# A hybrid mLSTM/GLA block with a PEER feed-forward: all activations computed ahead of the dense stage

## The chip, the core and the metric

The kernel runs on one core of a Trainium2 chip. The time is device microseconds of one execution of the whole program. The kernel before took 3271.71 us in the median of three runs (3260.62 to 3278.69).

## The reference, cut to what matters

One trunk layer over 1024 tokens of width 1024: a token mixer (two scans, mLSTM and gated linear attention, in both directions), and then a product-key feed-forward layer, PEER, whose experts are single neurons. The change is inside PEER and behind it.

```python
PEER_HEADS, PEER_NKEYS, PEER_TOPK = 8, 128, 16        # 128 * 128 = 16384 experts
def retrieve(xb):                                     # xb: 128 tokens x 1024
    q = (xb @ wq).reshape(128, 8, 2, 128)
    s = jnp.einsum('tphq,phkq->tphk', q, keys)        # 128 scores per head and half
    top_s, top_i = lax.top_k(s, 16)
    cand = top_s[:, :, 0, :, None] + top_s[:, :, 1, None, :]
    best_s, best_c = lax.top_k(cand.reshape(128, 8, 256), 16)
    ...
    idx = i1 * 128 + i2                               # 128 experts for each token
    g = jax.nn.softmax(best_s, axis=-1)
    act = jax.nn.gelu(jnp.einsum('tpkd,td->tpk', u_tab[idx], xb))
    return jnp.einsum('tpk,tpkd->td', g * act, v_tab[idx])
...
x = x + g2 * peer_ffn(h2, ...)
return rms_norm(x, norm_f_g)
```

Each token so uses 128 of the 16384 rows of U and of V, each 1024 long, in float32.

## The kernel before, in words

The front of the program (adaLN, projections, the scans, the output projection) runs to about 780 us and is the same in both kernels. PEER, function `peer`, then treats the eight blocks of 128 tokens in two ways.

*Gathered blocks.* Three blocks (`ng` = 3) fetch their rows. One **gather step** serves one of the 128 experts of each of 128 tokens: an indirect DMA on the POOL queue (L936) brings 128 rows of 8 KB (U and V side by side) into one of four buffers `uv`; VectorE multiplies the U half by the tokens and sums (L983, the dot); ScalarE applies gelu and the gate to one column `act` (L948, L949); VectorE adds `act` times the V half to the sum `acc` (L961, the add). There are 384 steps. In the query stage of the dense blocks every second dot's product is made by POOL (`share`, L981) and summed by ScalarE. The sum stands in PSUM (`accP`) up to the dense stage, and from there on in SBUF (`acc`).

*Dense blocks.* The other five blocks (640 tokens, `nd`) compute all experts, in 128 chunks of 128. For each chunk TensorE multiplies U by the 640 tokens (tile `ua`, 48 matmuls, each value as a high and a low float32r part, three products), ScalarE applies gelu (`w`); a table of gates G, made from the selected indices by one-hot matmuls (tile `gb`) and stored in DRAM as `d_G`, is multiplied in (L1376); the product is split into `wh` (ScalarE, L1379) and `wl` (VectorE, L1380); and TensorE multiplies it by V, half a row of 1024 at a time (L1403, tile `po`).

*Stages.* (1) queries and selection of the gathered blocks, to about 987 us; (2) queries and selection of the dense blocks, to 1370; (3) the table G, 80 pieces of 8 tokens, to 1832; (4) the last of the early activations; (5) the dense stage, from 1868 us. 84 of the 128 chunks (`early`) have their activations computed ahead of (5) and stored in DRAM as `d_A`; the other 44 are computed inside it.

*The order* is written out by the code itself; there is no scheduler in this part. A generator (`gather_all`) yields one gather step at a time. `dve(us, rate)` is called with an estimate of the VectorE work just recorded; it credits `rate` gather steps per microsecond, and records as many as are due (`ticks`). `fill` then records activation matmuls (a second generator) until an estimated TensorE clock is `lead` ahead of an estimated VectorE clock. So `rho` (query stage and selection), `rhog` (table) and `sige` (last activations) say how many gather steps stand beside each stage's work, and what is left of the 398 steps is spread over the dense stage: `share_of` per microsecond of matmul, times `ratio` in rounds of the first half of D.

*The dense stage.* Groups of 8 chunks (`GRP`) accumulate in PSUM: a **round** is one group and one half of D, five banks, one for each token block. In a round of the second half the weights of the next group are produced beside the matmuls (`produce`, `weights`). At the end of a round each bank is added to `accB` in SBUF (`v_add`: L1410, VectorE; in group 0 a copy by ScalarE, L1408). Six banks belong to these rounds and two to the `ua` products; so the second tile of a round needs a bank that the round before must have emptied. V arrives in pieces of 128 x 512 (`v_load`, L1348), ScalarE and POOL split each (`vh`, L1368, `vl`, L1369). U arrives in two halves per chunk (L1032), split by L1042 and L1043.

## Time and profile before

| | |
|---|---|
| median of three runs | 3271.71 us |
| profiled execution, its own time | 3258.37 us |
| its span, first to last instruction | 3256.6 us |
| mean granted TensorE clock | 0.945 |
| TensorE busy | 2895.9 us, 89% |
| VectorE busy | 2583.2 us, 79% |
| GpSimd busy | 1581.0 us, 49% |
| ScalarE busy | 1304.8 us, 40% |
| moved by DMA | 831.44 MB, mean 255 GB/s |

Busy time is the time in which an engine executes; what it waited for is shown by other views. Busy shares are averages over stages that differ, so the rows below are read by stage. Columns are explained where a view first appears.

### The profile page before, as it was taken

How to read it: one execution, taken by the hardware profiler on the slowest of the kernel's cores; microseconds unless marked ns; L12 is line 12 of the kernel's file. 1: busy time of each engine (PE TensorE's matmuls, PEld its weight loads, DVE VectorE, ACT ScalarE, POOL GpSimd, SP SyncE). 2: the span in 40 equal slices, each digit the busy share in tenths (PEclk: the TensorE clock that was granted, in tenths of full speed). 3: DMA queues.
4: the chain of work that ended last, by engine and by line, in shares of the span. 5: the costliest groups of instructions: out<-in, count | busy, mean ns of one | idle time of the engine just before them, and what ended most of it. 6: DMA issues, size and time to landing. Idle time of an engine off the chain costs nothing.

```text
span 3256.6 us, 47765 instructions
## 1 busy us (share of the span) xinstructions
PE 2895.9 (89%) x17321; PEld 2560.1 (79%) x17321; DVE 2583.2 (79%) x4467; ACT 1304.8 (40%) x2909; POOL 1581.0 (49%) x1102
## 2 busy tenths in 40 slices
PE   6999989998988987798888889989998899999897
PEld 3899887777988987688887877777777777778775
DVE  6633418666898999999999778888888788888886
ACT  4622224453444455455555433333333233333232
POOL 1000002333456766644343466666665566667664
PEclk9999999799998998899999999999999899999999
DMA  5254437345377876689898999999988898999883
GB/s 204 71 182 143 142 110 261 123 134 178 120 261 267 286 261 238 218 283 322 314 320 310 353 318 318 315 319 310 311 301 308 302 321 305 321 315 320 305 294 126
DMA packets 374381, 831.44 MB, mean 255 GB/s; under 512 B 27001, under 2 KB 198649, under 8 KB 324737
## 3 DMA queue, kind: packets, MB, share of 16 engines
q0 software_dynamic: 57600, 411.07, 35.0%
q1 hardware_dynamic: 292624, 347.74, 33.6%
q10 hardware_dynamic: 23920, 69.59, 5.5%
q8 instruction: 136, 2.23, 0.3%
q14 instruction: 101, 0.82, 0.1%
HBM read 729.38 MB, written 98.91 MB: 254 GB/s over the span
## 4 chain that ended last, share of the span: by engine, by line
DVE 21%; issue 11%; PE 10%; POOL 9%; DMA 5%; ACT 1%; SPq 0%; POOLq 0%; DVEq 0%; ACTq 0%
PE po L1403 7%; POOL vl L1369 4%; DVE ol L1296 4%; POOL uv L936 4%; DVE uv L983 4%; PE ua L1017 3%; DVE acc L961 3%; DMA uv<-uv,idx 3%; DVE accP L961 2%; DVE oh L1297 2%; DVE oh L1295 2%; DVE o L1294 2%; DVE w L1376 1%; DMA vr<-uv 1%; ACT wh L1379 1%
## 5 line engine op out<-in xcount | busy, mean ns | idle before, releaser
L936 POOL DMA_INDIRECT uv<-uv,idx x384 | 512.9, 1336 | 548.2 <-DVE accP L961 237.3
L983 DVE SCALAR_TENSOR_TENSOR uv<-uv,h2a 128x1024 f32<-128x1024 f32 x351 | 543.9, 1550 | 106.7 <-DMA uv<-uv,idx 106.5
L1403 PE MATMUL po<-vh,wh 128*128 128x512 f32 x1255 | 509.5, 406 | 118.4 <-DVE accB L1410 106.0
L1403 PE MATMUL po<-vl,wh 128*128 128x512 f32 x1255 | 507.1, 404 | 16.4 <-POOL vl L1369 16.4
L1017 PE MATMUL ua<-hBhi,uh 128*128 128x320 f32 x2048 | 487.2, 320 | 36.9 <-ACT uh L1042 30.3
L1403 PE MATMUL po<-vh,wl 128*128 128x512 f32 x1255 | 503.8, 401 | 0.0
L1017 PE MATMUL ua<-hBhi,ul 128*128 128x320 f32 x2048 | 478.4, 315 | 21.2 <-POOL ul L1043 20.9
L1369 POOL TENSOR_TENSOR vl<-vr,vh 128x512 fp32r<-128x512 f32 x251 | 387.2, 1545 | 198.4 <-ACT vh L1368 177.9
L1017 PE MATMUL ua<-hBlo,uh 128*128 128x320 f32 x2048 | 477.1, 315 | 0.0
L1043 POOL TENSOR_TENSOR ul<-ur,uh 128x512 fp32r<-128x512 f32 x256 | 391.9, 1553 | 171.3 <-ACT uh L1042 164.4
L961 DVE SCALAR_TENSOR_TENSOR acc<-uv,act,acc 128x1024 f32<-128x1024 f32 x237 | 398.3, 1681 | 8.5 <-ACT act L949 8.5
L1403 PEld LDWEIGHTS po<-vh,wh 128*128 128x128 f32 x1255 | 246.2, 196 | 179.8 <-DVE accB L1410 115.4
L1017 PEld LDWEIGHTS ua<-hBhi,uh 128*128 128x128 f32 x2048 | 352.0, 194 | 44.3 <-ACT uh L1042 32.9
L1017 PEld LDWEIGHTS ua<-hBhi,ul 128*128 128x128 f32 x2048 | 351.3, 193 | 26.9 <-POOL ul L1043 26.9
L1017 PEld LDWEIGHTS ua<-hBlo,uh 128*128 128x128 f32 x2048 | 352.6, 193 | 0.0
L1403 PEld LDWEIGHTS po<-vl,wh 128*128 128x128 f32 x1255 | 246.3, 196 | 72.0 <-POOL vl L1369 22.3
L1403 PEld LDWEIGHTS po<-vh,wl 128*128 128x128 f32 x1255 | 245.5, 196 | 53.0
L1379 ACT ACTIVATE wh<-w 128x640 fp32r<-128x640 f32 x128 | 94.6, 739 | 465.5 <-DVE w L1376 465.5
L1368 ACT ACTIVATE vh<-vr 128x512 fp32r<-128x512 f32 x251 | 156.5, 625 | 186.7 <-PE po L1403 156.1
L948 ACT ACTIVATE act<-act 128x1 f32<-128x1 f32 x384 | 76.1, 198 | 353.8 <-DVE uv L983 352.1
L468 POOL MEMSET v<- 128x4 f32 x20 | 2.0, 105 | 419.1 <-PE tm L207 383.7
L1380 DVE TENSOR_TENSOR wl<-w,wh 128x640 fp32r<-128x640 f32 x128 | 113.3, 885 | 104.8 <-ACT wh L1379 100.8
(375 smaller groups left out, 5920.5 us busy)
## 6 DMA issues: line engine op xcount, KB each, us to landing
ur<-uC SPq DMA_DIRECT2D x256, 256.0 KB
vr<-uv SPq DMA_DIRECT2D x256, 256.0 KB
d_G<-gtl ACTq DMA_DIRECT2D x80, 512.0 KB
gch<-d_G SPq DMA_DIRECT2D x64, 640.0 KB
d_A<-w ACTq DMA_DIRECT2D x84, 320.0 KB
w<-d_A SPq DMA_DIRECT2D x84, 320.0 KB
wm<-w_mod SPq DMA_DIRECT2D x32, 512.0 KB
qraw<-wq SPq DMA_DIRECT2D x32, 512.0 KB
```

Of the source, the lines that this page charges most:

```text
L936: G.indirect_dma_start(out=t.rearrange("p a d -> p (a d)"), out_offset=None, in_=A["uv"], in_offset=bass.IndirectOffsetOnAxis(ap=idxs[n][: ...
L948: S.activation(acts[i], acts[i], AF.Gelu)
L961: V.scalar_tensor_tensor(acc, v, act, acc, op0=ALU.mult, op1=ALU.add)
L983: V.scalar_tensor_tensor(t, t, 1.0, h2s[n], op0=ALU.mult, op1=ALU.mult, accum_out=acts[i])
L1017: T.matmul(pt[:, :b - a], l[:, kt], m[:, kt, a:b], start=(kt == 0 and wi == 0), stop=(kt == KT - 1 and wi == 2))
L1043: G.tensor_tensor(ul[:, k], ur, uh[:, k].bitcast(F32), op=ALU.subtract)
L1296: V.tensor_tensor(ol, oh, pairs(glT, b, t0), op=ALU.mult)
L1368: S.activation(vh, vr[n], AF.Copy)
L1369: G.tensor_tensor(vl, vr.pop(n), vh.bitcast(F32), op=ALU.subtract)
L1379: S.activation(wh, w, AF.Copy)
L1380: V.tensor_tensor(wl, w, wh.bitcast(F32), op=ALU.subtract)
L1403: T.matmul(po, st[:, b * P:(b + 1) * P], m, start=(start and wi == 0), stop=(stop and wi == 2))
```

## The change

- All 128 chunks have their activations computed ahead of the dense stage and stored in `d_A`; `early` and the code for the other case are gone. Those that are left after the table stage follow it in one loop. The dense stage multiplies by V alone.
- `GRP` = 8 becomes `GROUPS` = seven groups of 16 and two of 8.
- The sums of the gathered blocks stay in PSUM to the end: the two banks of `accP` belong to the whole function, in place of the two for `ua` in the dense stage.
- U is loaded and split a whole chunk at a time (128 x 1024), V two chunks of one half at a time (a new array `vC`, 4 KB runs), and G four chunks at a time.
- The first loads of the dense stage (three `d_A`, one G, three V) are issued ahead of the last activations.
- `weights` becomes a generator: w and wh first, wl at the next call.
- rho 0.42 to 0.58, rhog 0.33 to 0.43, ratio 1.35 to 4.0.

```diff
-GRP = 8
-NX = 5
+GROUPS = [16] * 7 + [8, 8]
+NX = 6
...
-def peer(tc, A, F, order, ng, out, ahi, alo, eh, ga, h2s, h2_load, early=84, rho=0.42, rhog=0.33, ratio=1.35, lead=6.0, sige=0.2):
+def peer(tc, A, F, order, ng, out, ahi, alo, eh, ga, h2s, h2_load, rho=0.58, rhog=0.43, ratio=4.0, lead=6.0, sige=0.2):
...
     def u_load(c):
-        if c < ulim[0] and c not in us:
-            us[c] = []
-            for k in (0, 4):
-                ur = ru[0].tile([P, 4, P], F32, tag="ru", name="ur")
-                Y.dma_start(ur, A["uC"][plan[c]][:, k:k + 4])
-                us[c].append(ur)
+        if c < P:
+            us[c] = ru.tile([P, KT, P], F32, tag="ru", name="ur")
+            Y.dma_start(us[c], A["uC"][c])
...
+    def activations():
...
+        for c in range(P):
+            pts = [bank("ua") for _ in cuts]
+            for n, d in enumerate(project(pts, None, *us.pop(c), bhi, blo, cuts)):
+                if n == 0:
+                    u_prep(c + 1)
+                if n == 1:
+                    u_load(c + 3)
+                yield d
+            w = up.tile([P, nd], F32, tag="we", name="w", bufs=3)
+            for pt, (a, b) in zip(pts, cuts):
+                S.activation(w[:, a:b], pt[:, :b - a], AF.Gelu)
+            S.dma_start(d_A[c], w)
...
-    owed, spare = [0.0], [(early - 4) * KT // 2]
+    owed, spare = [0.0], [(P - 4) * KT // 2]
...
+        pc = es.enter_context(tc.tile_pool(name="pc", bufs=1, space=PSUM))
         pb = esp.enter_context(tc.tile_pool(name="pb", bufs=6, space=PSUM))
-        pc = esp.enter_context(tc.tile_pool(name="pc", bufs=1, space=PSUM))
...
+    for c in range(3):
+        a_load(c)
+    g_load(0)
+    for n in range(0, 6, 2):
+        v_load(n)
+    for d in earlier:
+        clock["PE"] += d
+        ticks(d, sige)
+    v_prep(0)
     eru.close()
...
-    for n in list(accs):
-        if accs[n] is psum[0]:
-            settle(n)
-    psum.clear()
...
             V.tensor_tensor(w3, w3, gts[c // 4][:, :, c % 4], op=ALU.mult)
             wh = wp.tile([P, nd], F32R, tag="wh", name="wh")
+            S.activation(wh, w, AF.Copy)
+            yield
             wl = wp.tile([P, nd], F32R, tag="wl", name="wl")
-            S.activation(wh, w, AF.Copy)
             V.tensor_tensor(wl, w, wh.bitcast(F32), op=ALU.subtract)
...
         def produce(c):
...
-            if c not in first:
-                for d in u_side(plan.index(c), True):
-                    ticks(d, share_of)
-            pend.append(c)
+            a_load(c + 3)
+            if c % 4 == 0:
+                g_load(c + 4)
+            pend.append(weights(c))
...
-        share_of = max(steps[0] - 12, 0) / (ratio * mm + mm + (P - early) * KT * 3 * nd / 2400.0)
+        some = sum(GROUPS[:-1]) + GROUPS[0]
+        many = sum(GROUPS[1:-1])
+        share_of = max(steps[0] - 12, 0) / ((ratio * many + some) * nb * t1)
...
+                rate = share_of * (ratio if g and not h else 1.0)
...
+    A['vC']=f(i['peer_v'][0].reshape(64,2,128,2,512).transpose(0,3,2,1,4))
```

What this does to the order is seen in the built programs. Counted there, of the 384 adds of the gather steps 77 stand before the table stage, 62 in it, 9 from there to the first weights and 236 behind them; after the change 105, 82, 44 and 153. Of the 128 chunks of activations 79 stand before the end of the table stage, 8 more before the first V matmul, and 41 behind it; after it 94.25, 33.75 and none.

VectorE in the dense stage before the change, from the end of a second-half round into a first-half round (`uv` and `acc` rows are a gather step's dot and add, `gch` a part of G, `po` a bank):

```order
L1376 TENSOR_TENSOR w_22056<-w_22056,gch_22058 128x640
L1380 TENSOR_TENSOR wl_22214<-w_22056,wh_22213 128x640
L1410 TENSOR_TENSOR accB_19123<-accB_19123,po_21750 128x512
L1410 TENSOR_TENSOR accB_19123<-accB_19123,po_21751 128x512
L1410 TENSOR_TENSOR accB_19123<-accB_19123,po_21752 128x512
L1410 TENSOR_TENSOR accB_19123<-accB_19123,po_21753 128x512
L1410 TENSOR_TENSOR accB_19123<-accB_19123,po_21754 128x512
L983 SCALAR_TENSOR_TENSOR uv_22131,act_22245<-uv_22131,h2a_17103 128x1024
L961 SCALAR_TENSOR_TENSOR acc_19127<-uv_22063,act_22172,acc_19127 128x1024
L1376 TENSOR_TENSOR w_22093<-w_22093,gch_22058 128x640
L1380 TENSOR_TENSOR wl_22259<-w_22093,wh_22258 128x640
L983 SCALAR_TENSOR_TENSOR uv_22168,act_22275<-uv_22168,h2a_17103 128x1024
```

The same engine after the change, where the weights of a second-half round end and the gather steps of a first-half round begin (`accP` is the sum in PSUM):

```order
L1363 TENSOR_TENSOR wl_22934<-w_22837,wh_22926 128x640
L983 SCALAR_TENSOR_TENSOR uv_22726,act_22958<-uv_22726,h2a_14968 128x1024
L961 SCALAR_TENSOR_TENSOR accP_8048<-uv_22632,act_22829,accP_8048 128x1024
L1358 TENSOR_TENSOR w_22865<-w_22865,gch_22758 128x640
L983 SCALAR_TENSOR_TENSOR uv_22825,act_22983<-uv_22825,h2a_14968 128x1024
L961 SCALAR_TENSOR_TENSOR accP_8048<-uv_22726,act_22958,accP_8048 128x1024
L1363 TENSOR_TENSOR wl_22986<-w_22865,wh_22971 128x640
L983 SCALAR_TENSOR_TENSOR uv_22954,act_23007<-uv_22954,h2a_14968 128x1024
L961 SCALAR_TENSOR_TENSOR accP_8048<-uv_22825,act_22983,accP_8048 128x1024
L983 SCALAR_TENSOR_TENSOR uv_22979,act_23032<-uv_22979,h2a_14968 128x1024
L961 SCALAR_TENSOR_TENSOR accP_8048<-uv_22954,act_23007,accP_8048 128x1024
```

From there the gather steps go on without another instruction between them to the five adds of `po`: between two such adds stand 17 gather steps and one weight, or 5 gather steps and 15 weights, by turns. Before, the two kinds had 6 or 7 and 1, or 8 to 10 and 7.

SP's queue at the end of the table stage, before the change (`ur` is U, `w<-d_A` stored activations, `gch` G, `vr` V):

```order
L909 DMA out<-ft 128x1024
L1032 DMA ur<-uC 128x512 x10
L1340 DMA w<-d_A 128x640
L1032 DMA ur<-uC 128x512 x2
L1334 DMA gch<-d_G 128x10x128
L1348 DMA vr<-uv 128x512 x5
```

And after it:

```order
L909 DMA out<-ft 128x1024
L1027 DMA ur<-uC 128x1024 x30
L1312 DMA w<-d_A 128x640 x3
L1306 DMA gch<-d_G 128x10x256
L1319 DMA vr<-vC 128x1024 x3
L1027 DMA ur<-uC 128x1024 x31
```

The first loads of the dense stage stood behind the early chunks' U; now 31 loads of U follow them.

## Rows read from the trace of the kernel before

**Rows 1.** The page: busy time, share of the span and instructions of each engine.

```profile
PE 2895.9 (89%) x17321; PEld 2560.1 (79%) x17321; DVE 2583.2 (79%) x4467; ACT 1304.8 (40%) x2909; POOL 1581.0 (49%) x1102
```

**Rows 2.** Busy time by stage: stretch, length, engines, clock, DMA share, GB/s.

```profile
987.00:1155.00 168.00, 160.75 (x1097) 157.99 (x1098) 159.57 (x710) 78.71 (x199) 122.45 (x74) 0.98 0.80 280
1155.00:1370.00 215.00, 163.87 (x996) 157.54 (x995) 210.83 (x529) 105.72 (x217) 139.74 (x91) 0.88 0.70 241
1370.00:1832.00 462.00, 400.34 (x3320) 385.47 (x3320) 454.99 (x518) 265.20 (x459) 192.31 (x148) 0.96 0.87 307
1832.00:1868.00 36.00, 34.44 (x235) 34.18 (x234) 17.18 (x20) 13.92 (x37) 21.30 (x16) 1.00 0.96 370
```

**Rows 3.** One line's instructions, V matmuls: duration ns min/median/max, first and last start us.

```profile
L1403 PE MATMUL po<-vh,wh x1255: 387/389/796, 1895.8 to 3239.9; 128*128 128x512 f32 x180
```

**Rows 4.** The chain that ended last, around 1940 us: start, length, what.

```profile
1939.51 7.04 PE ua L1017 x48
1946.55 10.24 PE po L1403 x45
```

**Rows 5.** Who waited for whom, 1896 to 3170 us: total us, times, longest.

```profile
PE po L1403 <- DVE accB L1410: 101.0, 20, 7.8
...
DVE wl L1380 <- ACT wh L1379: 95.2, 116, 2.0
DVE uv L983 <- DMA uv<-uv,idx: 86.0, 53, 4.1
```

**Rows 6.** Busy time of `uv`'s instructions alone, by stage: VectorE, ScalarE, GpSimd.

```profile
987.00:1155.00 168.00, 67.90 (x69) 19.55 (x34) 78.82 (x53) 0.98 0.80 280
...
1370.00:1832.00 462.00, 158.05 (x189) 0.00 (x0) 72.70 (x63) 0.96 0.87 307
...
1896.00:3170.00 1274.00, 753.78 (x696) 0.00 (x0) 332.32 (x232) 0.95 0.90 311
```

**Rows 7.** Who waited for whom, SP's queue, the whole span.

```profile
SPq L1340 <- DMA d_A<-w: 24.3, 1, 24.3
```

**Rows 8.** Groups by line, VectorE, 1896 to 3170 us; last row 987 to 1155.

```profile
L961 DVE SCALAR_TENSOR_TENSOR acc<-uv,act,acc 128x1024 f32<-128x1024 f32 x231 | 389.5, 1686 | 1.7 <-ACT act L949 1.7
L983 DVE SCALAR_TENSOR_TENSOR uv<-uv,h2a 128x1024 f32<-128x1024 f32 x232 | 385.1, 1660 | 86.1 <-DMA uv<-uv,idx 86.0
...
L1376 DVE TENSOR_TENSOR w<-w,gch 128x640 f32<-128x640 f32 x121 | 148.8, 1229 | 6.7 <-ACT w L1058 6.7
...
L1380 DVE TENSOR_TENSOR wl<-w,wh 128x640 fp32r<-128x640 f32 x121 | 107.3, 887 | 99.2 <-ACT wh L1379 95.2 <-issue 4.0
...
L961 DVE SCALAR_TENSOR_TENSOR accP<-uv,act,accP 128x1024 f32<-128x1024 f32 x35 | 45.3, 1294 | 8.4 <-ACT act L949 8.4
```

**Rows 9.** Timeline of VectorE: start us, us, instruction, idle before it.

```profile
2003.24 2.31 DVE L983 SCALAR_TENSOR_TENSOR uv<-uv,h2a 128x1024 f32<-128x1024 f32 x1
...
2007.62 1.37 DVE L983 SCALAR_TENSOR_TENSOR uv<-uv,h2a 128x1024 f32<-128x1024 f32 x1 [0.87 <-DMA uv<-uv,idx]
...
2013.64 1.22 DVE L983 SCALAR_TENSOR_TENSOR uv<-uv,h2a 128x1024 f32<-128x1024 f32 x1 [3.44 <-DMA uv<-uv,idx]
...
2017.09 1.23 DVE L983 SCALAR_TENSOR_TENSOR uv<-uv,h2a 128x1024 f32<-128x1024 f32 x1 [1.02 <-DMA uv<-uv,idx]
...
2019.44 3.07 DVE L1410 TENSOR_TENSOR accB<-accB,po 128x512 f32<-128x512 f32 x5
```

**Rows 10.** Timeline of GpSimd, the same stretch.

```profile
2001.24 1.69 POOL L936 DMA_INDIRECT uv<-uv,idx  x1 [1.35 <-DVE acc L961]
2002.96 1.51 POOL L1369 TENSOR_TENSOR vl<-vr,vh 128x512 fp32r<-128x512 f32 x1
2004.62 1.76 POOL L936 DMA_INDIRECT uv<-uv,idx  x1
...
2008.05 1.77 POOL L936 DMA_INDIRECT uv<-uv,idx  x1
```

**Rows 11.** The chain that ended last, the same stretch.

```profile
2008.05 9.02 DMA uv<-uv,idx
```

## Blind prediction

> **What bounds the kernel now.** I read the busy times by stage first, then the starts of the V matmuls, then who waits for whom inside the dense stage, and last the order of single instructions there. Up to 900 us the change touches nothing, so the sum starts with the first gather.
>
> Over the whole span TensorE is the busiest engine [rows 1], but that is an average. From 987 to 1832 us, in the query, select and table stages, VectorE is busy 160 of 168, 211 of 215 and 455 of 462 us, while TensorE has room in the last two [rows 2]: these stages are as long as VectorE's list. From 1832 us until the first V matmul at 1895.8 [rows 3] TensorE works through the last of the early activations, at 7.04 us for a chunk of 48 matmuls; a V unit (one chunk, one half of D, 15 matmuls) takes 10.24/3 = 3.41 us [rows 4]. From 1895.8 to 3256.6 lies the dense stage, 1361 us. There TensorE waits 101 us for VectorE to empty the PSUM banks, in 20 waits. VectorE itself waits only for ScalarE's copy wh (95 us) and for gathered rows (86 us), and for TensorE in none of the rows [rows 5]: it is always behind. So before the change the dense stage is VectorE's list too, with the waits in it.
>
> **The change part by part.** Gathers are counted by the adds, and chunks by the matmuls, in the built order of both kernels.
>
> *Query to table stage.* rho and rhog put 105 gathers in place of 77 ahead of the table stage and 82 in place of 62 into it. A gather costs VectorE 67.9/35 = 1.94 us in the query stage, where POOL takes half of the products, and 158/63 = 2.51 us in the table stage [rows 6]. That makes 28 x 1.94 + 20 x 2.51 = 105 us, on the path since VectorE is full there. In this time TensorE does 15.25 chunks more (94.25 in place of 79), which is 107 us of its work: what is paid here is taken out of the dense stage later. If the small idle times of VectorE (8 + 4 + 7 us) and shorter waits for POOL absorb part, it is 75; if the added gathers cost the 3.25 us of the dense stage, it is 155. I take 107.
>
> *Activation stage.* Before, 63.6 us from 1832 to the first V matmul hold 8 chunks (56.3 us), so 7 us are lost. After, 33.75 chunks stand there: 238 us at 7.04. VectorE has 44 gathers in it, some 120 us, and is covered. On SP the first loads of the weights now stand ahead of the last 31 loads of U, and the first of them waits until the table stage's last stores are out; the same load waited 24.3 us before [rows 7]. Two loaded chunks and the one in work cover some 17 us of it. I charge 5 us for that and 6 for the start of the dense stage: 249 in place of 64, so +185. With the cover complete it is 6 less, without any 17 more.
>
> *Dense stage.* Activations leave it altogether (41 chunks, 289 us of TensorE). 153 gathers are left of 236. Each cost VectorE 753.8/232 = 3.25 us here [rows 6]. The sum now stays in PSUM. An add into SBUF took 1.69 us here, an add into PSUM 1.29 us in the query stage, where POOL was 73% busy [rows 2, 8]. Dense PSUM adds are not in the trace, so the price lies between 1.29 and 1.69; I take 1.29, since no stage before shows the PSUM form slower, and get 2.86 a gather (the other end costs 61 us more). A chunk's weights cost 1.23 + 0.89 us and a wait of 95.2/121 = 0.79 for wh: 2.9 us [rows 5, 8]. The five adds of a round cost 3.07 us [rows 9].
>
> There are now seven groups of 16 and two of 8, so 18 rounds in place of 32. TensorE needs 54.6 us for a round of 16. The built order gives a second-half round 15 weights and 5 gathers, and a first-half round 1 weight and 17 gathers. Second half: 15 x 2.9 + 5 x 2.86 - 5 x 0.79 (a gather between w and wl hides the wait) + 3.1 = 57 us. The two rounds of group 0 come to 57 each as well.
>
> First half: VectorE's own work would be 17 x 2.86 + 2.9 + 3.1 = 54.6 us, just TensorE's. But it needs a gather every 54.6/17 = 3.2 us, and here I look at how fast gathers come. Four buffers hold them, and each is asked for when the buffer four steps earlier is free, two steps before it is used; so a step can't be shorter than half the time from issue to landing. Where the old order has five gather steps in a row, the dots start at 2003.24, 2007.62, 2013.64 and 2017.09, with waits for the DMA of 0.87, 3.44 and 1.02 us [rows 9]. The three that were waited for had been issued at 2001.24, 2004.62 and 2008.05, so they took 6.3, 9.0 and 9.0 us; the chain has the last one with 9.02 [rows 10, 11]. Half the mean is 4.05; the steps themselves average 4.6. Between gathers POOL did a vl of 1.5 us; it will do one of two halves for every two units, so the issue is delayed less often. I take 4.0 a step. Three gathers are there at the start: 3 x 2.86 + 14 x 4.0 + 5 = 69 us. The bounds are 57 (gathers on time) and 3 x 2.86 + 14 x 6.02 + 5 = 98 (each step like the longest one shown).
>
> The sum: 2 x 57, 6 x 69, 5 x 57, then 56 (second half with 8 weights), 34 and 31 and 31 (the rounds of 8 with 8, 3 and 0 gathers), 27 for the last half and 16 from the last V matmul (3239.9, rows 3) to the end: 1008 us. That is 353 less.
>
> **A page against the rows.** A gather of 128 rows of 8 KB is 1.049 MB. The Trainium skill (DMA: Bandwidth & Descriptors, section on the anatomy of one DMA on the gpsimd path) gives a DMA issued from GpSimd about 2.0 us and its bytes at 436 GB/s. As an estimate from that page, 4.4 us; the trace does not agree in this stretch (6.3 to 9.0 us). By that rule gathers would keep pace, and the time would be the first rival's.
>
> The second place is the PSUM add. Rows 8 show the two-SBUF-input forms at 1.66 and 1.69 us in the dense stage and the PSUM form at 1.29 us. The Trainium skill (SBUF — State Buffer, section on who interferes with whom) says that a VectorE instruction with two inputs in SBUF competes with a GpSimd instruction that reads SBUF, and one with a single SBUF input does not. By it the PSUM adds stay at 1.29; without it the 61 us above come back. It also says that the one that starts first holds the port for its whole instruction, which speaks against the longer POOL subtractions of this change; no run here shows by how much.
>
> **Sum.** 107 + 185 - 353 = -61 us. The span would be 3196, its own time (1.8 us more) 3197. The profiled execution of before took 3258.4, 13.3 below the median of the runs; I carry that over: 3211 us.
>
> **The rivals.**
>
> *Gathers keep pace.* Then the six first-half rounds take 57 and the short one 30: 932 us, 76 less, so 3135. For it: first-half rounds carry no weights and no U, so the DMA engines have less else to do, and V comes in longer runs. Against it: the five-in-a-row stretch carried only gathers and V as well.
>
> *Gather steps as slow as in the old runs.* At 4.5 to 4.87 us the first-half rounds grow to 77 to 82, and what the change moves around is worth nothing: 3255 to 3288. For it: the 4.6 us of the three steps shown. Against it: POOL's queue, which held up those issues, gets shorter.
>
> *Slower.* Place: the same first-half rounds; mechanism: with 17 gathers in a row more of them are in flight at once, POOL reaches each issue late behind a subtraction twice as long, and the step grows past 4.87 us. Then 89 limited steps (6 x 14 + 5) cost more than the 77 us that separate 3211 from 3288; at 5.3 us the time is 3211 + 89 x 1.3 = 3327. For it: the step of 6.02. Against it: a wait this long has appeared only now and then.
>
> **How the numbers follow.** The forecast (steps of 3.6 to 4.45 us, 3175 to 3250) gets 0.45, gathers on time 0.27, no change 0.15, slower 0.13. Half a percent, about what a measurement of this kernel can tell from no change, is 16 us, so faster means under 3255 and slower over 3288. Faster 0.45 + 0.27 = 0.72, same 0.15, slower 0.13. The range has to take in most of the first rival and the no-change case: 3120 to 3290.
>
> **What would show it.** Right: the table stage ends near 1940 us, the first V matmul starts near 2188, first-half rounds last about 69 us and second-half rounds 57, with VectorE waiting for gathered rows for some 15 us in each first-half round and TensorE waiting that long at its end; adds into PSUM at 1.29 us. Wrong: VectorE's waits for gathers stay under 40 us in all (first rival), or exceed 200 us (slower); the PSUM adds take 1.6 us; TensorE has gaps of over 20 us at the start of the activation stage, since the loads of U stood behind those of the weights.

## The result and the profile after

The change made the kernel slower: 3319.52 us (median of 4 runs, 3314.11 to 3321.36) against 3268.47 us in the runs of before beside them, a ratio of 1.0152 [1.0119, 1.0184]. The profiled execution has a span of 3312.3 us, where the forecast had 3196. The first answer to [rows 1] is that TensorE does the same 17321 matmuls in 54 us more, and VectorE 137 us less:

```profile
PE 2949.5 (89%) x17321; PEld 2579.9 (78%) x17321; DVE 2445.9 (74%) x4373; ACT 1298.0 (39%) x2682; POOL 1442.2 (44%) x861
```

So the expected relief of VectorE came, and the time went elsewhere. The stages show where. Columns are stretch and length, then the busy time of TensorE, its loads, VectorE, ScalarE and GpSimd, then clock, DMA share and GB/s. First before, cut at the same events as after (first ua matmul, first and last matmul of the remaining rows' query, first gb matmul, end of gb, first V matmul, end):

```profile
870.50:987.00 116.50, 94.86 (x612) 93.34 (x612) 105.82 (x339) 50.83 (x90) 57.61 (x43) 0.90 0.68 233
987.00:1136.50 149.50, 143.31 (x978) 140.80 (x979) 141.07 (x622) 68.06 (x171) 108.74 (x64) 0.98 0.80 281
1136.50:1376.90 240.40, 188.22 (x1156) 181.52 (x1155) 235.04 (x625) 118.28 (x248) 157.46 (x103) 0.89 0.70 241
1376.90:1831.20 454.30, 392.64 (x3274) 377.87 (x3274) 448.49 (x511) 262.48 (x454) 188.32 (x145) 0.96 0.88 309
1831.20:1895.80 64.60, 58.93 (x385) 57.86 (x385) 32.96 (x36) 24.40 (x58) 35.40 (x25) 0.97 1.00 371
1895.80:3256.60 1360.80, 1213.56 (x5809) 1036.87 (x5807) 1136.74 (x1175) 428.39 (x1058) 882.52 (x578) 0.95 0.87 299
```

And after:

```profile
877.20:1008.70 131.50, 108.89 (x685) 106.22 (x685) 119.65 (x350) 54.48 (x90) 64.42 (x35) 0.91 0.70 249
1008.70:1205.70 197.00, 174.09 (x1122) 170.97 (x1123) 175.38 (x645) 85.18 (x213) 143.52 (x82) 0.91 0.81 284
1205.70:1500.20 294.50, 227.35 (x1347) 219.65 (x1346) 279.64 (x653) 134.34 (x273) 189.24 (x103) 0.86 0.74 256
1500.20:2004.50 504.30, 442.35 (x3599) 423.48 (x3598) 493.60 (x568) 282.49 (x475) 222.11 (x130) 0.97 0.92 332
2004.50:2268.30 263.80, 241.50 (x1621) 240.57 (x1620) 113.06 (x132) 79.72 (x191) 130.09 (x76) 0.95 0.87 315
2268.30:3312.30 1044.00, 943.27 (x3840) 741.89 (x3840) 780.40 (x865) 308.70 (x611) 541.62 (x290) 0.95 0.83 300
```

The three stages ahead of the tables grew from 506.4 to 623.0 us (+116.6), the table stage by 50.0, the activation stage by 199.2, and the dense stage shrank by 316.8. The first ua matmul stands 6.7 us later, in code that is the same; over the kernels below it stands at 874 to 893, so this is the spread between executions.

In the dense stage, VectorE's waits [rows 5] are these, one row being one releaser with its total, times and longest:

```profile
DVE uv L983 <- DMA uv<-uv,idx: 111.1, 61, 4.5
DVE wl L1363 <- ACT wh L1360: 109.1, 114, 5.2
```

and TensorE's:

```profile
PE po L1383 <- DVE accB L1390: 49.6, 13, 7.3
PE po L1383 <- POOL vl L1329: 33.0, 24, 2.8
```

Before, the same two rows over the whole stage read

```profile
PE po L1403 <- DVE accB L1410: 106.0, 21, 7.8
PE po L1403 <- POOL vl L1369: 16.4, 13, 3.4
```

The waits for the PSUM banks halved, about as the rounds did, and those for vl doubled. The adds answer [rows 8]: they cost in the dense stage what they cost in the query stage (duration in ns, least, median and most):

```profile
L961 DVE SCALAR_TENSOR_TENSOR accP<-uv,act,accP x152: 1274/1280/1290, 2279.8 to 3233.7; 128x1024 f32<-128x1024 f32 x152
```

By its po matmuls the dense stage splits into rounds: 65.4 and 56.0 us for group 0; 68.4, 68.2, 68.3, 67.6, 67.1 and 65.6 for the first halves of groups 1 to 6; 67.8, 65.7, 58.9, 61.2, 62.2 and 62.5 for their second halves.

### The profile page after: what moved, and what is told of

The parts are those of the page before. It is cut to its first block, busy times and chain, and to the rows that moved or that the text cites. A ratio compares the mean times of both kernels' runs of the same rounds, so it can differ in the third digit from the quotient of the medians.

```text
span 3312.3 us, 46430 instructions
## 1 busy us (share of the span) xinstructions
PE 2949.5 (89%) x17321; PEld 2579.9 (78%) x17321; DVE 2445.9 (74%) x4373; ACT 1298.0 (39%) x2682; POOL 1442.2 (44%) x861
## 3 DMA queue, kind: packets, MB, share of 16 engines
q1 hardware_dynamic: 221056, 362.15, 32.5%
## 4 chain that ended last, share of the span: by engine, by line
DVE 16%; PE 14%; issue 13%; POOL 7%; DMA 3%; ACT 1%; ACTq 0%; POOLq 0%; SPq 0%; DVEq 0%
PE ua L1017 7%; PE po L1383 7%; DVE oh L1285 4%; POOL vl L1329 3%; POOL uv L936 3%; DVE accP L961 3%; DVE uv L983 3%; DVE o L1282 2%; DVE ol L1284 1%; DVE oh L1283 1%; DMA uv<-uv,idx 1%; DVE wl L1363 1%; ACT wh L1360 1%; DVE w L1358 1%; POOL ul L1034 1%
## 5 line engine op out<-in xcount | busy, mean ns | idle before, releaser
L936 POOL DMA_INDIRECT uv<-uv,idx x384 | 480.5, 1251 | 627.0 <-DVE accP L961 467.0
L983 DVE SCALAR_TENSOR_TENSOR uv<-uv,h2a 128x1024 f32<-128x1024 f32 x339 | 502.0, 1481 | 210.7 <-DMA uv<-uv,idx 210.4
L961 DVE SCALAR_TENSOR_TENSOR accP<-uv,act,accP 128x1024 f32<-128x1024 f32 x381 | 488.2, 1281 | 97.8 <-ACT act L949 95.5
L1017 PE MATMUL ua<-hBhi,uh 128*128 128x320 f32 x2048 | 494.4, 323 | 67.3 <-ACT uh L1033 58.0
L1017 PE MATMUL ua<-hBhi,ul 128*128 128x320 f32 x2048 | 487.9, 321 | 65.1 <-POOL ul L1034 65.1
L1329 POOL TENSOR_TENSOR vl<-vr,vh 128x1024 fp32r<-128x1024 f32 x125 | 318.7, 2550 | 272.1 <-ACT vh L1328 256.4
L1034 POOL TENSOR_TENSOR ul<-ur,uh 128x1024 fp32r<-128x1024 f32 x128 | 323.2, 2526 | 195.3 <-ACT uh L1033 118.8
L1363 DVE TENSOR_TENSOR wl<-w,wh 128x640 fp32r<-128x640 f32 x128 | 166.0, 1297 | 109.1 <-ACT wh L1360 109.1
L1266 ACT ACTIVATE gtl<-gb 128x512 f32<-128x512 f32 x160 | 161.1, 1113 | 48.5 <-PE gb L1264 35.7
```

Source lines behind the costliest of these rows:

```text
L936: G.indirect_dma_start(out=t.rearrange("p a d -> p (a d)"), out_offset=None, in_=A["uv"], in_offset=bass.IndirectOffsetOnAxis(ap=idxs[n][: ...
L961: V.scalar_tensor_tensor(acc, v, act, acc, op0=ALU.mult, op1=ALU.add)
L983: V.scalar_tensor_tensor(t, t, 1.0, h2s[n], op0=ALU.mult, op1=ALU.mult, accum_out=acts[i])
L1017: T.matmul(pt[:, :b - a], l[:, kt], m[:, kt, a:b], start=(kt == 0 and wi == 0), stop=(kt == KT - 1 and wi == 2))
L1034: G.tensor_tensor(ul, us[c], uh.bitcast(F32), op=ALU.subtract)
L1266: S.activation(gt[:, :, tt:tt + 4].rearrange("p e t -> p t e"), pt.rearrange("p (t e) -> p t e", e=P), AF.Copy, scale=1.0 / 4096.0)
```

## The experiments

Twelve kernels ran, each beside runs of the kernel before. Times are medians; ratios are against before, so the changed kernel's is 1.0152. Lengths of stages are those of one profiled execution of each kernel.

### e1_u_halves: one part undone, the split of U

```
+ for k in (slice(0, 4), slice(4, 8)):
+     S.activation(uh[:, k], us[c][:, k], AF.Copy)
+     G.tensor_tensor(ul[:, k], us[c][:, k], uh[:, k].bitcast(F32), op=ALU.subtract)
```

> The changed kernel, with U split into its high and low parts in two halves of 128x512 again (ScalarE and GpSimd), loads unchanged. Up to the table stage the changed kernel lost 114 us where 55 were expected; each added gather cost about 4 us there. Theory L: the longer subtraction of U on GpSimd (2.5 us in place of 1.5) holds up VectorE instructions with two SBUF inputs for longer; then these stages shorten by 20 to 40 us and the time is 3280 to 3300. Theory N (rival): the gathers themselves are that dear there (product on GpSimd, sum on ScalarE, add waiting for it), whatever the form of the U split; then the time stays within 8 us of 3319.

Measured: 3339.17 us, 1.0203 [1.0169, 1.0236]. The longer subtraction is not what slowed the stages ahead of the tables: they last 623.0 us with it and 623.6 with halves. The table stage with halves takes 525.8 us in place of 504.3. Theory L falls; if anything the long form is the better one. Theory N is right about the early stages, but the time missed its range too (within 8 us of 3319), by what the table stage grew.

### e2_rho_old: the early gathers undone

```
- rho=0.58, rhog=0.43
+ rho=0.42, rhog=0.33
```

> The changed kernel with the old rates of gather steps beside the early stages (rho 0.42, rhog 0.33), everything else as changed. Theory N: the stages from the first gather to the end of the table return to their old length within 10 us (962 us from 870 to 1832), since the number of gathers is what made them longer. Theory L: 20 to 40 us of the loss stay there. In both, some 15 chunks go back to the activation stage (+107 us) and about 28 gathers more reach the dense stage at 3 to 4 us each (85 to 110 us), so the time is 3340 to 3365 by N and 3365 to 3400 by L. If it comes out under 3319 an early gather costs more than a late one.

Measured: 3341.52 us, 1.0202 [1.0161, 1.0243]. Its stages (same columns and cuts) are the key to the sum:

```profile
1158.90:1398.90 240.00, 188.62 (x1156) 182.79 (x1154) 232.98 (x625) 116.28 (x224) 150.28 (x79) 0.89 0.69 240
1398.90:1846.20 447.30, 391.69 (x3276) 376.97 (x3275) 440.80 (x511) 259.90 (x414) 176.86 (x104) 0.96 0.88 314
1846.20:2216.20 370.00, 350.89 (x2353) 349.30 (x2351) 166.44 (x192) 116.55 (x278) 192.38 (x112) 0.97 0.89 317
2216.20:3350.70 1134.50, 966.68 (x3840) 751.04 (x3840) 861.22 (x949) 323.39 (x667) 572.55 (x318) 0.93 0.83 302
```

The stages ahead of the tables are back at 506.1 us with 77 gathers in them (106 in the changed kernel): the 29 cost 116.9 us, 4.0 each. The table stage is back at 447.3 with 63 (82): 57 us for 19, 3.0 each. What that saves, 174 us, is lost again: 15.25 chunks and 20 gathers are left over for the activation stage (+106) and 28 gathers for the dense stage (+90, 3.2 each). The time is at the lower end of theory N's range. So early gathering is no gain or loss that can be told (the two intervals overlap); by its own figures the forecast had it as a gain, because it took 1.94 for 4.0.

### e3_late_loads: the loads of the dense stage behind the activation stage's

The first loads of weights, tables and V are issued 40 steps into the loop over the last activations, not ahead of it.

```
  for i, d in enumerate(earlier):
      clock["PE"] += d
      ticks(d, sige)
+     if i == 40:
+         for c in range(3):
+             a_load(c)
+         g_load(0)
...
```

> The changed kernel with the first loads of the dense stage issued ten chunks into the activation loop, in place of ahead of it. Theory S: SP stood at the first of these loads until the table stage's last stores were out, the loads of U behind it came late, and TensorE had one gap of 16 us for it; then the gap goes and the time falls by 10 to 16 us, to about 3305. Rival: the gap only moves (the next U load or the dense stage's first weights come late instead), and the time stays within 4 us of 3319.

Measured: 3298.25 us, 1.0074 [1.0049, 1.0099]. In the changed kernel, from 1990 to 2060 us, SP's queue stood at a load for the table stage's last store, and TensorE for U behind it (a row of each engine's waits):

```profile
SPq L1312 <- DMA d_G<-gtl: 36.2, 4, 32.5
...
PE ua L1017 <- ACT uh L1033: 16.2, 1, 16.2
```

With the late loads the second row reads

```profile
PE ua L1017 <- ACT uh L1033: 3.2, 1, 3.2
```

and the activation stage takes 250.9 in place of 263.8 us. Theory S's gap is gone but for 3.2 us, and did not move elsewhere. These 13 us are shown. The ratio went down by 0.8% (25 us), more than the 10 to 16 us of theory S; what the rest is the profile does not say. The two profiled executions differ by 4.8 us only: that of e3 is its slowest, that of the changed kernel its fastest.

### e4_interleave: the weight product of the next chunk ahead of the last chunk's subtraction

On VectorE the order w(c), wl(c-1), w(c+1), wl(c) takes the place of w(c), wl(c), w(c+1), wl(c+1). For that, the weights of three chunks are begun ahead of the dense stage's loop in place of two.

```
- def weigh():
-     if pend and next(pend[0], True):
-         pend.pop(0)
+ def weigh(b):
+     if b == 1 and pend:
+         half.append(pend.pop(0))
+         next(half[-1])
+     ...
+     elif len(half) > (1 if more[0] else 0):
+         next(half.pop(0), None)
```

> The changed kernel with the weights of two chunks interleaved on VectorE: w of a chunk stands ahead of wl of the chunk before it, so that ScalarE's wh is done when wl's turn comes. Theory V: the second-half rounds (62 to 68 us where 57 were expected and TensorE needs 54.6) are as long as VectorE's list, in which 114 waits for wh take 109 us; then those waits fall under 30 us, these rounds come to 56 to 59 us, and the time falls by 35 to 60 us, to 3260 to 3285. Rival P: these rounds are set by the V split on GpSimd and the DMA; then the waits for wh turn into others, and the time stays within 10 us of 3319.

Measured: 3309.48 us, 1.0112 [1.0078, 1.0147]. VectorE's waits in the dense stage:

```profile
DVE uv L983 <- DMA uv<-uv,idx: 116.3, 69, 5.8
DVE accP L961 <- ACT act L949: 53.3, 18, 10.6
DVE w L1358 <- DMA w<-d_A: 48.8, 24, 7.9
DVE wl L1363 <- ACT wh L1360: 18.2, 11, 5.7
```

The wait for wh fell from 109.1 to 18.2 us, and two others grew by 35 (accP, from 18.5) and 49 (w): a wait taken out was handed on. Theory V falls: the second-half rounds of groups 1 to 5 took 311 us in place of 316. The waits did what rival P said, and the time is at the edge of its 10 us; that GpSimd's split of V and the DMA set these rounds, as P has it, is not shown by this.

### e5_ratio, e6_hold, e7_sige: the round's two halves, its end, and gathers moved into the activation stage

```
e5:  - ratio=4.0           + ratio=1.35
e6:  - if nxt and i == len(group) - 1 and b >= HOLD:
     + if nxt and (i > len(group) - 3 or i == len(group) - 3 and b >= HOLD):
e7:  - sige=0.2            + sige=0.25
```

What e6 aims at is the end of a round. On VectorE, in the changed kernel:

```profile
2595.88 1.22 DVE L983 SCALAR_TENSOR_TENSOR uv<-uv,h2a 128x1024 f32<-128x1024 f32 x1 [4.02 <-DMA uv<-uv,idx]
...
2598.94 1.22 DVE L983 SCALAR_TENSOR_TENSOR uv<-uv,h2a 128x1024 f32<-128x1024 f32 x1 [0.62 <-DMA uv<-uv,idx]
...
2600.09 1.28 DVE L961 SCALAR_TENSOR_TENSOR accP<-uv,act,accP 128x1024 f32<-128x1024 f32 x1
2601.28 3.07 DVE L1390 TENSOR_TENSOR accB<-accB,po 128x512 f32<-128x512 f32 x5
```

and on TensorE at that time:

```profile
2602.02 0.79 PE L1383 MATMUL po<-vh,wh 128*128 128x512 f32 x1 [5.75 <-DVE accB L1390]
2602.61 0.63 PE L1383 MATMUL po<-vl,wh 128*128 128x512 f32 x1
2603.03 0.63 PE L1383 MATMUL po<-vh,wl 128*128 128x512 f32 x1
...
2607.26 0.39 PE L1383 MATMUL po<-vh,wh 128*128 128x512 f32 x1
2607.50 0.39 PE L1383 MATMUL po<-vl,wh 128*128 128x512 f32 x1
```

The granted clock of TensorE is the column in front of the DMA share, here 0.50 and then 1.00:

```profile
2602.00:2607.20 5.20, 5.18 (x12) 4.12 (x13) 5.20 (x8) 0.00 (x0) 2.96 (x2) 0.50 1.04 388
2607.30:2612.00 4.70, 4.70 (x22) 3.80 (x21) 2.27 (x3) 1.74 (x3) 0.00 (x0) 1.00 0.87 315
```

VectorE has two gathers in its list ahead of the adds that empty the banks, and sits 4 us for a row. TensorE stands 5.75 us; then its matmuls start 0.43 us apart for some 5 us, at the lower of its two clock levels (1.2 GHz), then 0.23 at the upper one (2.4 GHz). That costs about 2 us more.

> The changed kernel with ratio=1.35 as in the kernel before, in place of 4.0: the gathers of the dense stage are spread nearly evenly over the two halves of a round pair (about 12.6 and 9.4 in place of 17.6 and 4.4). Theory R (a first-half round of 66 to 68 us is the gathers' own pace: with four row buffers a gather can be fetched only when the one four back is added, 4.2 us each, and 16 of them make 67 us): 12.6 gathers no longer fill the round, first halves come down to 58 to 61 us; the second halves, with 9.4 gathers at 2.83 us and 16 weight chunks at 2.23 us, grow from 63 to 65 to 68. A pair of rounds stays within 4 us of the 128 us it has, and the whole within 3290 to 3325. Rival D (VectorE's sum of work sets the second halves and every gather moved there is added whole): second halves of 75 us or more, 3340 to 3370. Rival E (spread gathers wait for no transfer at all and the pair falls to 118): 3250 to 3270.

> The changed kernel, but no gather step is issued in the last three chunks of a round (before: in the last chunk after its first block); they are made up at the start of the next round. Theory B (at the end of a round the five adds of the PSUM banks stand on VectorE behind two gathers, one of which waits up to 4 us for its row; TensorE waits 2 to 7 us for them, since only one of the six banks is spare, and then runs some 4 us at half clock): 13 round ends give back 3 to 5 us each, the waits of TensorE for the accB adds fall from 50 us to under 15, and the time to 3260 to 3285. Rival R (a first-half round is as long as its 16 gathers at 4.2 us; what is held over only moves the same wait into the next round): first-half rounds stay at 66 to 68, second-half rounds lose 3 at most, 3300 to 3325.

> The changed kernel with sige=0.25 in place of 0.2: a quarter more gather steps per us of matmul in the activation stage (about 54 gathers there in place of 43, the dense stage has 142 in place of 153). Theory S (TensorE bounds the activation stage, VectorE is idle for 145 of its 264 us, so the gathers there cost nothing; in the dense stage each costs up to 4.2 us of a first-half round): activation stage within 264 plus or minus 6, dense stage 20 to 40 shorter, 3280 to 3300. Rival Q (GpSimd's queue orders a gather's issue and its wait ahead of the subtraction that the next chunk needs, as VectorE's rows come late): the activation stage grows by 15 to 30 and eats the gain, 3310 to 3335.

Measured: e5 3297.87 us, 1.011 [1.0082, 1.0138]; e6 3325.84 us, 1.0203 [1.0162, 1.0244]; e7 3298.7 us, 1.0111 [1.008, 1.0142].

e5: with 12 gathers in place of 16 the first-half rounds of groups 2 to 6 fell from 67.4 to 63.4 us, and the second halves, with 8 or 9 in place of 6 or 7, went from 62.1 to 60.8. In group 0, which now has some 8 gathers a round in place of 4, the two rounds grew from 121.4 to 133.1. The time is in theory R's range, but its rounds are not as it had them: the first halves stayed above its 58 to 61, and the second halves did not grow to 65. e6: theory B failed, and the time is just over rival R's range, so the hold alone gains nothing (its interval and the changed kernel's overlap). The bank waits fell nearly as far as B had said, but the vl waits, 33.0 before, took their place:

```profile
PE po L1383 <- POOL vl L1329: 62.1, 43, 3.5
PE po L1383 <- DVE accB L1390: 15.4, 6, 4.3
```

e7: 11 gathers went from the dense into the activation stage, which takes 269.9 us (+6); the dense stage takes 1010.6 (-33, 3.0 a gather). All three are in theory S's ranges.

### e8_all: five edits together

e3's and e4's edits, ratio=1.6, e6's hold and sige=0.25.

> The changed kernel with five edits together: the first loads of the dense stage are issued 40 steps into the activation loop; the weight product of the next chunk stands ahead of the subtraction of the last on VectorE; ratio=1.6; no gather step in the last three chunks of a round; sige=0.25. If the round ends, the gathers' pace and the loads are separate causes, the gains add: 3320 less 21 (loads), less 10 (order), less 30 to 45 (round ends), less 20 to 35 (gathers moved into the activation stage): 3210 to 3240, under the kernel before. If they are one and the same wait, shown at several places, it is the best of the single ones: 3270 to 3300.

Measured: 3245.43 us, 0.9941 [0.9912, 0.997], ahead of the kernel before. By the ratios the single edits changed the time by -25, -13, -14 (at 1.35), +17 and -13 us, 48 in all; together they gave 69, with the intervals some 10 us each. That is neither the full sum of the expectation (3210 to 3240) nor the best single edit (3270 to 3300). The hold, of no use alone, may gain once the gathers are spread; no run took it out of the five. TensorE's waits in the dense stage, now 977.8 us:

```profile
PE po L1394 <- POOL vl L1329: 26.4, 25, 3.7
...
PE po L1394 <- DVE accB L1401: 4.7, 3, 2.0
```

### e9_share0: no GpSimd products in the query and selection stages

```
- share[0] = 2
+ share[0] = 0
```

> The kernel of e8_all, with share 0 in place of 2 in the query and selection stage of the remaining rows: there every gather's product is made by VectorE; before, every second one was made by GpSimd (a 128x1024 product of two SBUF operands). It asks why the 29 gathers added to these two stages cost 4.0 us each and not the 1.94 that the forecast took. In e8_all the stretch from the first ua matmul to the first gb matmul is 620.5 us. Theory C (GpSimd's products take the port from VectorE's two-operand instructions: about 53 products, each holding up a VectorE instruction by 1.9 us, and the add waits for ScalarE's sum of the product): without them VectorE gains more than the 1.3 us that a product of its own costs; the stretch falls by 15 to 50 us, to 570 to 605, and the time with it. Rival F (VectorE's own work is the price and contention is small): 53 products of 1.3 to 1.5 us come on top, the stretch grows by 30 to 75 us, to 650 to 695, and the time to 3275 to 3320.

Measured: 3244.64 us, 0.9922 [0.9892, 0.9952]. The stretch took 630.6 us: between the two theories, and with 8.5 more chunks in it, because the code that writes the order counts VectorE's longer list. The time is that of e8_all, and the run does not decide between the theories by it. The selection stage shows more. First e8_all, its stage and its products on VectorE, and one of the other instructions there:

```profile
1200.50:1495.00 294.50, 225.72 (x1348) 217.78 (x1348) 280.80 (x653) 134.24 (x273) 189.17 (x103) 0.87 0.74 256
...
L983 DVE SCALAR_TENSOR_TENSOR uv<-uv,h2a 128x1024 f32<-128x1024 f32 x25 | 39.4, 1575 | 0.0
L835 DVE TENSOR_TENSOR oh<-r,rjb 128x2048 bf16<-128x2048 bf16 x5 | 25.7, 5147 | 0.0
```

and e9_share0:

```profile
1219.50:1508.30 288.80, 250.00 (x1565) 243.99 (x1564) 267.75 (x686) 114.48 (x239) 141.84 (x81) 0.91 0.76 271
...
L983 DVE SCALAR_TENSOR_TENSOR uv<-uv,h2a 128x1024 f32<-128x1024 f32 x49 | 76.8, 1568 | 2.0 <-DMA uv<-uv,idx 2.0
L835 DVE TENSOR_TENSOR oh<-r,rjb 128x2048 bf16<-128x2048 bf16 x5 | 18.1, 3622 | 0.0
```

VectorE does 24 products more, 37.4 us, and is still busy 13.1 us less: its other work went from 241.4 to 190.9 us. Some 5 of these 50 us are rows that e9's stretch has fewer of. So 24 GpSimd products had cost VectorE's other instructions some 45 us there, 1.9 each, more than the 1.57 of a product of its own. One mask of the changed kernel shows how. Undisturbed, in the first stage of the kernel before, this instruction takes 1.22 us; here it took 8.00, through one product and two subtractions of GpSimd in a row (until 1374.52) and 1.1 us more:

```profile
1367.62 8.00 DVE L835 TENSOR_TENSOR oh<-r,rjb 128x2048 bf16<-128x2048 bf16 x1
...
1367.55 2.37 POOL L981 TENSOR_TENSOR uv<-uv,h2a 128x1024 f32<-128x1024 f32 x1
1369.86 4.66 POOL L1034 TENSOR_TENSOR ul<-ur,uh 128x1024 fp32r<-128x1024 f32 x2
```

In the query stage it was less: VectorE's busy time rose by 17.6 us for 21 products, which at 1.49 each are 31 us, so that GpSimd's had cost some 14 us there, 0.7 each.

### e10_v512: the split of V in pieces of 512 again

```
- vh = vp.tile([P, 2, 512], F32R, tag="vh", name="vh")
+ vh = vp.tile([P, 512], F32R, tag="vh", name="vh", bufs=4)
- v_prep(n + 2)
+ v_prep(n + 3)
```

(and vl alike)

> The kernel of e8_all, with V's halves made in pieces of 512 columns in four buffers each, three pieces ahead (same memory), in place of pieces of 1024 in two buffers, two pieces ahead: the longer runs of V undone for the split, not for the loads. In the dense stage of e8_all (973.8 us) TensorE waits 25 times, 26 us in all, for a vl of GpSimd, and runs some us at half clock behind each. Theory G (a pair of 1024 columns can be begun only when TensorE is done with the pair two back, and then has 6.8 us for a ScalarE copy, GpSimd's queue with a gather's issue waiting in it, and 2.4 us of subtraction; with four pieces of 512 it has 10 us and half the work): the vl waits fall under 8 us and the dense stage by 20 to 45, to 3200 to 3225. Rival O (twice as many GpSimd instructions, 125 more of them, meet VectorE's two-operand instructions more often and each has its start cost): the waits go but VectorE loses 1.1 us per meeting; dense stage within 10 of 973.8, 3235 to 3255.

Measured: 3249.39 us, 0.9934 [0.9916, 0.9951]. The dense stage takes 977 us as before:

```profile
PE po L1395 <- DVE accB L1402: 16.4, 7, 4.0
PE po L1395 <- POOL vl L1330: 10.0, 12, 2.0
```

The vl waits fell by 16 us and the bank waits rose by 12. Rival O's time, but by a wait handed on, not by more meetings of GpSimd and VectorE: VectorE's busy time in the stage went from 763.4 to 756.7 us.

### e11_seven and e12_rho42: towards a better kernel

e11 joins e8, e9 and e10 with sige=0.30; e12 is e11 with rho=0.42.

> The kernel of e8_all with both edits of e9_share0 (no GpSimd products in the query and selection stage) and e10_v512 (V split in pieces of 512), and sige=0.30 in place of 0.25, since only some 25 chunks are left for the activation stage in e9_share0 and 41 gathers fit in it. Theory M (in e9_share0 the stages before the dense one are 35 us shorter than in e8_all, and the dense stage 42 longer for its 14 more gathers; a gather in the activation stage is free up to one per 4.2 us, so about 8 come back; and the vl waits, 46 us in e9_share0, fall to some 10): activation stage 206 plus or minus 5 with 48 to 50 gathers, dense stage 975 to 1000, time 3215 to 3235. Rival W (a wait taken away is handed on, as in e6_hold and e10_v512): the time of e8_all, e9_share0 and e10_v512, 3240 to 3255.

> The kernel of e11_seven with rho=0.42 as in the kernel before, in place of 0.58: about 25 gathers leave the query and selection stages for the dense stage, rhog stays. Theory P (a gather there costs 4.0 us of the stage, as in the changed kernel against the kernel before, one in the dense stage 3.1, from e7_sige): the two stages 100 us shorter, the dense stage 78 longer, and the chunks that VectorE's shorter time leaves undone, some 4 to 7 at 7.04 us, 28 to 50 us on the activation stage: within 30 of e11_seven, and slower rather than faster. Rival C (without GpSimd's products the early gathers cost their own 2.8 us and no more): the stages 70 shorter, dense 78 and activation 28 to 50 longer: 35 to 60 slower than e11_seven.

Measured: e11 3234.94 us, 0.9882 [0.9856, 0.9908]; e12 3223.64 us, 0.9839 [0.981, 0.9869], the lowest median of all, 1.6% under before, though its interval overlaps that of e11. e11 came out at the upper edge of theory M: the activation stage had its 48 gathers, but took 219 us in place of 206. In e12 28 gathers left the first three stages (78 in place of 106), which fell from 624.4 to 530.6 us, 3.4 each, between the prices of the two theories. The activation stage grew by 93 us, for 10.75 chunks, but took 21 of the gathers; the dense stage got only 8 more and grew by 25. Both theories had sent all of the freed gathers to the dense stage. Theory C's 35 to 60 us of loss did not come; theory P's range (within 30 us) held, but its "slower rather than faster" did not. Where the medians' gain of 11 us lies the stages do not show: the profiled execution of e12, its slowest, is 10.7 us longer than that of e11, one of its fastest.

## Why the prediction was wrong

The forecast and the trace, step by step:

| step | forecast | measured |
|---|---|---|
| first three stages, 29 gathers more | +54 (28 x 1.94) | +116.6 |
| table stage, 20 gathers more | +50 (20 x 2.51) | +50.0 |
| activation stage | 249 | 263.8 |
| dense stage | 1008 | 1044.0 |

**The step that failed: "A gather costs VectorE 67.9/35 = 1.94 us in the query stage".** It is the mean of the gather's own VectorE instructions, taken as the price of one more. The price was 4.0 (e2 took them out and got it back), above even the upper bound, which took 3.25. The forecast hung on it. By its own terms the change without the added early gathers is slower than before: 107 us of chunks and 28 gathers at 2.86 to 4.0 us go back behind the tables, and only 107 us are saved ahead of it, so -61 becomes +19 to +51. e2, at 2.0% over the kernel before, is 66.

What the 116.6 us for the 29 gathers consist of can be read from the gathers' own instructions (tile `uv`) in the three stages, the sum before and after:

```profile
sum 506.40, DVE 155.75 ACT 37.96 POOL 178.77; mean DVE 51.92 ACT 12.65 POOL 59.59
...
sum 623.00, DVE 237.63 ACT 51.77 POOL 244.49; mean DVE 79.21 ACT 17.25 POOL 81.50
```

These rows of VectorE grew by 81.9 us, 2.8 a gather in place of 1.94: four of the 29 stand in the first stage, where VectorE makes all products, and in the query stage the mean of its dots rose from 1483 to 2047 ns. VectorE's other instructions grew by 10.9 us, and its idle time by the last 23.9. e9 shows one cause of the longer instructions: half of the gathers of the query and selection stages send GpSimd a product that holds them up, by some 0.7 and 1.9 us for each product. That is not the whole price: in e11 and e12, which send no such products, an early gather still cost 3.4 us. Where the idle time comes from, no run shows.

A rival is left open too. The prediction called the query stage as long as VectorE's list, but TensorE was busy for 143.3 of its 149.5 us as well. With the 11 gathers added there came three chunks, 21 us of TensorE at the prediction's 7.04, in a growth of 47.5 us. No run added gathers without chunks, so the 4.0 us is the price of a gather with what the code that writes the order puts beside it.

In the table stage, which sends GpSimd no products, the same way of costing gave 50 for a measured 50.0, in part by luck: against e2, which also has the long subtractions of U, 19 gathers cost 57 us there, 3.0 each and not 2.51, and e2's stage was 7 us shorter than that of before.

The Trainium skill (SBUF — State Buffer, section on who interferes with whom) says that VectorE instructions with two inputs in SBUF compete with GpSimd instructions that read SBUF. e9 agrees, with some 45 us for 24 products. The prediction used that rule for the PSUM adds, where it held (1.280 us), and did not apply it to what the added gathers send to GpSimd. Its words that an instruction with a single SBUF input does not compete are too wide for this case: L823, which reads one operand, took 1807 ns on the mean in e8_all's selection stage and 220 in e9's. What it drew from the same section against long subtractions is not borne out: e1, with halves, has the longer table stage.

**Activation stage, 15 us over.** Here the right sign had been named (U's loads behind the weights' loads, a gap of over 20 us as the wrong sign), and 5 us were charged. The gap was 16.2 us; e3 took 13 of it away. The cover of two loaded chunks did not last, since the load ahead stood 32.5 us for the last table store, not the 24.3 of [rows 7].

**Dense stage, 36 us over.** The time of the first-half rounds was right: six of them take 405 us (forecast 414), with the dots of group 3's 3.8 us apart (15 steps from 2666.90 to 2724.19) and the wait for rows there 14.8 us. The other sign, TensorE waiting about as long at the end of such a round, did not come: it stood 2.2 to 7.3 us there. In group 3's it also stood 4.8 us for vl, and its matmuls were busy for 60.2 us where a round without a stop, the second of group 0, takes 56.0. The second-half rounds of groups 1 to 5 took 316 us in place of 285, that of group 6 62.5 in place of 56, and group 0's two 121 in place of 114. For them VectorE's work was summed, as if it could run as one list beside TensorE; it stops TensorE at the round's end and GpSimd stops it at a vl, and of the 17 stops of over 2 us in the stage all but one are followed by matmuls at the lower clock, which cost 1.1 to 2.5 us more. e6 and e10 show that neither stop is the cause by itself: when one goes, the other grows. How the 36 us divide between them is not shown.

**The slower rival had the right sign and the wrong place.** It wanted gather steps of over 4.87 us; they were at 3.8. Over half of the miss came from stages to which no rival had been given. With 60 us over the 107 that were taken up to the end of the table stage, 14 in the activation stage, 36 in the dense one and 7 of spread, the 117 us over the forecast's span are accounted for.

## What to carry to other kernels

Price one more instruction by what its whole step does to the stage, its orders to other engines included, not by the mean of its own rows; two executions with different numbers of it, or a neighbouring stage with and without such orders, give that. Work moved early is only a gain where the stage it moves into has an idle engine for it: here the activation stage, where VectorE was busy for 113 of 264 us, took 11 gathers for 6 us in e7, and the selection stage, where VectorE was busy for 235 of 240, took 4 us for each. In a tight pipeline a single wait removed can move to the next one, so edits should be tried together before one is thrown out.

## What was not expected of the hardware

A GpSimd product of 128x1024 (about 2.4 us) lengthened VectorE's other instructions by some 1.9 us in the selection stage: the 128x2048 mask at L835 went from 5147 to 3622 ns on the mean when the products were gone. A single one of these stood through three GpSimd instructions in a row, 8.00 us in place of 1.22. After a stop of 5.75 us TensorE started its next ten or so matmuls 0.43 us apart in place of 0.23, so that the stop cost about a third more than its length. Cutting GpSimd's subtractions of U in two left its own time in the table stage the same (49 of 2613 ns, 98 of 1340), and that stage was 21 us longer.
